# The first FFN part's gate and value products, from SBUF copies to work in their PSUM banks

## The chip, the cores and the metric

The kernel runs on one core of one Trainium2 chip. The time is that of one execution on the device, in microseconds (us). A change below about 0.5% (7.6 us) can hardly be told from none here.

## What is computed

One inference step of a decoder layer on 1032 tokens (a prompt of 1024 and 8 single samples), d_model 1024, everything in fp32. Four recurrent mixers (S5, mLSTM, GLA, RWKV-7) work side by side on 256 channels each, then a gated feed-forward network (FFN) with a causal depthwise convolution of width 3 on the gate. The change touches the FFN alone, whose reference is

```python
h2 = rmsnorm(x, norm_ffn)
up = (h2 @ ffn_w_up).astype(F32)            # 1024 -> 2*2816
ug, uv = jnp.split(up, 2, axis=-1)
padded = jnp.concatenate([ffn_buf.astype(F32), ug], axis=1)
conv = ffn_conv_b.astype(F32)
for j in range(CONV_W):
    conv = conv + ffn_conv_w[j] * padded[:, j:j + T]
ffn = (jax.nn.gelu(conv) * uv) @ ffn_w_down # 2816 -> 1024
x = x + ffn.astype(x.dtype)
```

## The kernel before

**Products.** Activations are kept feature-major: 128 features on the partitions, tokens along the row. An fp32 product is made of three passes in a shorter format (`mm3`, L1123): weights and activations are each split into a high part and a rest, and TensorE adds wh·high (L1129), wh·rest (L1130) and wl·high (L1131) in one PSUM bank. A weight block (128 x 1024) is loaded and split by `load_w`: an SP DMA, a cast on ACT (L1111), four subtractions on POOL (L1112), two buffers of each kind. Activations are split by `split_act`: a cast on ACT (L1120), a subtraction on DVE (L1121).

**Stages.** The tokens go in two segments, 0 to 512 and 512 to 1032. The mixers of the first segment run first, with the input products. Then comes the first FFN part, `ffn(k,0,512,...)`, together with the mixers of the second segment (`SEQ1`); TensorE does FFN work where the mixers leave it free. When the mixers are done (the last mixer matmul is at 981 us) the first FFN part is finished, and the second segment's output product and FFN (`gate_last`) follow, up to the end.

**The first FFN part.** 22 blocks of 128 hidden features, j = 0 to 21. For each, `gate_first` makes a gate product and a value product (`up`, 24 matmuls of 512 columns each) and returns the gated value, which `split_act` splits for the down product; `down(n)` multiplies the blocks by groups of four and adds to the residual `xa` (L1295). `gate_first` before:

- three SBUF tiles from the pool "t" (`tt`, 5 slots): `acc`, `t`, `qr`;
- the gate product in bank `p`; ACT writes the convolution's first tap and the bias to `acc` (L1306), DVE adds the two others from the bank (L1307, twice), ACT keeps the last two columns (L1308);
- the value product in bank `q`; ACT copies it to `qr` (L1310), POOL multiplies it by `acc` (L1311);
- the gelu's gate, `gelu_gate`: Square on ACT (L124), two DVE steps (L125, L126), a sigmoid of three ACT steps (L119 to L121);
- DVE multiplies the two (L1313) into `acc`, which is returned; then L1120 and L1121.

**PSUM.** The FFN and the other big products take banks in turn from a pool of three (`psg`, tag "g"); the other five banks belong to the mixers (`psm`, tags ma, mb, mc).

**Order.** The program is written with priorities (`PRI`: mixers before FFN, and weight loads by a count of their own); a scheduler of the framework puts each engine's instructions into one fixed order at build time, by its own estimate of when they are ready. An instruction waits on its engine, and all behind it on that engine wait too.

Of the kernel before, what the change touches and what calls it, by code (L numbers as in the profile page):

```python
# [8 lines left out]
AF=mybir.ActivationFunctionType; ALU=mybir.AluOpType; PSUM=bass.MemoryType.PSUM; DRAM=bass.MemoryType.DRAM  # L9
# [107 lines left out]
def sigmoid_(k,o,scale=-1.0):  # L117
    A=k.nc.scalar
    A.activation(out=o,in_=o,func=AF.Exp,scale=scale)  # L119
    A.activation(out=o,in_=o,func=AF.Ln,bias=k.eps[0:o.shape[0],2:3])  # L120
    A.activation(out=o,in_=o,func=AF.Exp,scale=-1.0)  # L121
def gelu_gate(k,t,x):

    k.nc.scalar.activation(out=t,in_=x,func=AF.Square,scale=0.044715**.5)  # L124
    k.nc.vector.scalar_tensor_tensor(out=t,in0=t,scalar=1.0,in1=x,op0=ALU.add,op1=ALU.mult)  # L125
    k.nc.vector.tensor_scalar(out=t,in0=t,scalar1=-27.0,scalar2=None,op0=ALU.max)  # L126
    sigmoid_(k,t,-1.5957691216057308)
def v1(k,name,i): 
    c=VC[name]+i
    return k.vec[:,c:c+1]  # L130
# [968 lines left out]
def load_w(k,src,tags=None):  # L1099

    nc=k.nc; k.wn+=1
    if tags: r=k.wp.tile([128,1024],F32,tag="wr",name="wr",bufs=k.wb[0]); h,l=[k.ga.tile([128,1024],F32R,tag=n,name=n) for n in tags]
    elif k.w3 and k.wn%3==0: r,h,l=[k.ga.tile([128,1024],t,tag=n,name=n) for n,t in (('p0',F32),('p1',F32R),('p2',F32R))]
    else: r,h,l=[k.wp.tile([128,1024],t,tag=n,name=n,bufs=b) for n,t,b in zip(('wr','wh','wl'),(F32,F32R,F32R),k.wb)]
    shp=src.shape; n=int(np.prod(shp[1:]))
    def view(t):
        v=t[:,0:n]
        return v if len(shp)==2 else v.rearrange("p (a b)->p a b",a=shp[1]) if len(shp)==3 else v.rearrange("p (c a b)->p c a b",c=shp[1],a=shp[2])
    with k.pr('S'):
        nc.sync.dma_start(out=view(r),in_=src)  # L1110
        nc.scalar.copy(h[:,0:n],r[:,0:n])  # L1111
        for c in range(0,n,256): nc.gpsimd.tensor_tensor(out=l[:,c:c+256],in0=r[:,c:c+256],in1=h[:,c:c+256].bitcast(F32),op=ALU.subtract)  # L1112
    return view(h),view(l)

def tt(k): return k.tp.tile([128,HW],F32,tag="t",name="t",bufs=k.tb)
# [17 lines left out]
def chunks(N):  # L1133
    return [(0,N)] if N<=512 else [(0,N//2),(N//2,N)]
# [44 lines left out]
def split_gain(k,N,i,x,gname):  # L1179
    h=htile(k,i); g=v1(k,gname,i)  # L1180
    k.nc.scalar.activation(out=h[:,0,0:N],in_=x,func=AF.Identity,scale=g)  # L1181
    k.nc.vector.scalar_tensor_tensor(out=h[:,1,0:N],in0=x,scalar=g,in1=h[:,0,0:N].bitcast(F32),op0=ALU.mult,op1=ALU.subtract)  # L1182
    return h

def split_norm(k,N,i,x,r,gname):

    t=tt(k)[:,0:N]; k.nc.gpsimd.tensor_tensor(out=t,in0=x,in1=r[:,0:N],op=ALU.mult)
    return split_gain(k,N,i,t,gname)
# [91 lines left out]
def ffn(k,c0,c1,x2,rs,last=False,then=None):  # L1280
    nc=k.nc; V=nc.vector; A=nc.scalar; GP=nc.gpsimd; N=c1-c0
    NP=N-8
    hs=[split_gain(k,N,i,x2[i][:,0:N],'nffn') if last else split_norm(k,N,i,x2[i][:,0:N],rs.rstd(),'nffn') for i in range(8)]; ms=None if last else Ms(k,N)
    ch=chunks(N); o=2*last
    hid={}
    def down(n):
        ph=[hid.pop(j) for j in range(max(4*n-o,0),min(4*n-o+4,22))]; end=n==5; nm=8//len(ph)
        wd=lambda i,tags=None: load_w(k,(k.wdn,k.wdl)[last][max(4*n-o,0)+i].rearrange("p (m k c)->p m k c",m=nm,c=128),tags)
        if last and end: return ffn_last(k,c0,x2,ch,ph,[wd(0),wd(1),wd(2,("h0","h1")),wd(3,("h2","h3"))])
        for m in range(8):  # L1290
            if m%nm==0: w=wd(m//nm)
            for a,b in ch:
                p=gps(k)
                mm3(k,p[:,0:b-a],(w[0][:,m%nm],w[1][:,m%nm]),ph,a,b)
                V.tensor_tensor(out=x2[m][:,a:b],in0=x2[m][:,a:b],in1=p[:,0:b-a],op=ALU.add)  # L1295
            if end: ms.add(x2[m][:,0:N])
    def up(w):
        ps=[]
        for a,b in ch:
            p=gps(k); ps.append(p)  # L1300
            mm3(k,p[:,0:b-a],w,hs,a,b)
        return ps
    def gate_first(j,wg,wv):

        acc=tt(k); t=tt(k); qr=tt(k); p=up(wg)[0]
        A.activation(out=acc[:,0:N],in_=p[:,0:N],func=AF.Identity,scale=v1(k,'cw2',j),bias=v1(k,'cb',j))  # L1306
        for o,n in ((1,'cw1'),(2,'cw0')): V.scalar_tensor_tensor(out=acc[:,o:N],in0=p[:,0:N-o],scalar=v1(k,n,j),in1=acc[:,o:N],op0=ALU.mult,op1=ALU.add)  # L1307
        A.copy(k.halo[:,j],p[:,N-2:N])  # L1308
        q=up(wv)[0]
        A.copy(qr[:,0:N],q[:,0:N])  # L1310
        GP.tensor_tensor(out=qr[:,0:N],in0=acc[:,0:N],in1=qr[:,0:N],op=ALU.mult)  # L1311
        gelu_gate(k,t[:,0:N],acc[:,0:N])
        V.tensor_tensor(out=acc[:,0:N],in0=qr[:,0:N],in1=t[:,0:N],op=ALU.mult)  # L1313
        return acc
    def gate_last(j,wg,wv):
        g=k.tp.tile([128,HW+2],F32,tag="t",name="t",bufs=k.tb); acc=tt(k)
        pg=up(wg); r=rs.rstd()
        for (a,b),p in zip(ch,pg): V.tensor_tensor(out=g[:,2+a:2+b],in0=p[:,0:b-a],in1=r[:,a:b],op=ALU.mult)  # L1318
        pv=up(wv)
        A.activation(out=acc[:,0:N],in_=g[:,2:2+N],func=AF.Identity,scale=v1(k,'cw2',j),bias=v1(k,'cb',j))  # L1320
        GP.tensor_copy(g[:,0:2],k.halo[:,j])
        V.scalar_tensor_tensor(out=acc[:,0:NP],in0=g[:,1:1+NP],scalar=v1(k,'cw1',j),in1=acc[:,0:NP],op0=ALU.mult,op1=ALU.add)
        V.scalar_tensor_tensor(out=acc[:,0:NP],in0=g[:,0:NP],scalar=v1(k,'cw0',j),in1=acc[:,0:NP],op0=ALU.mult,op1=ALU.add)
        V.tensor_tensor(out=acc[:,NP:N],in0=acc[:,NP:N],in1=k.sdec[:,j],op=ALU.add)
        GP.tensor_copy(k.fcd[:,j],g[:,2+NP:2+N])
        GP.tensor_copy(k.halo[:,j],g[:,NP:NP+2])
        A.activation(out=acc[:,0:N],in_=acc[:,0:N],func=AF.Gelu_apprx_tanh)
        if j==21: k.tc.keep_in_program_order(A.preload_act_table_set("natural_log_exp_and_others"))
        GP.tensor_tensor(out=acc[:,0:N],in0=acc[:,0:N],in1=r[:,0:N],op=ALU.mult)
        for (a,b),q in zip(ch,pv): V.tensor_tensor(out=acc[:,a:b],in0=acc[:,a:b],in1=q[:,0:b-a],op=ALU.mult)  # L1330
        return acc

    for j in range(22):
        wg=load_w(k,k.wup[j,0]); wv=load_w(k,k.wup[j,1])
        acc=(gate_last if last else gate_first)(j,wg,wv)
        u="p%d"%(j-14 if last and j>18 else j%5); h=(k.xb if u>"p4" else k.ga).tile([128,2,HW],F32R,tag=u,name=u)
        split_act(k,h,N,acc[:,0:N]); hid[j]=h
        if j==21 if last and j>=18 else j%4==o and j: down(min((j-1)//4,4))
        if j==1 and then: then()
    if last: return down(5)  # L1340
    def rest():
        now=k.psg,k.tp,k.tb; k.psg,k.tp,k.tb=own[:3]
        down(5); own.append(ms.rstd())
        k.psg,k.tp,k.tb=now
    own=[k.psg,k.tp,k.tb]
    return rest,lambda: ffn_end(k,c0,c1,x2,own[3])

def ffn_last(k,c0,x2,ch,ph,w):

    nc=k.nc; V=nc.vector; A=nc.scalar  # L1350
    def out(a,b,ms):
        n=b-a; r=ms.rstd()
        with k.pr('G'): mul(a,b,n,r)
    def mul(a,b,n,r):
        for m in range(8):
            if m%2==0: t=k.tp.tile([128,2,n],F32,tag="yo",name="yo",bufs=6)
            x=x2[m][:,a:b]; o=t[:,m%2]
            if m in(1,4,6): nc.gpsimd.tensor_tensor(out=o,in0=x,in1=r[:,0:n],op=ALU.mult)
            else: V.scalar_tensor_tensor(out=o,in0=x,scalar=v1(k,'nfin',m),in1=r[:,0:n],op0=ALU.mult,op1=ALU.mult)  # L1359
            if m%2: nc.sync.dma_start(out=k.yT[(m-1)*128:(m+1)*128,c0+a:c0+b].rearrange("(m p) c->p m c",p=128),in_=t)  # L1360
    done=None; ch=((0,LC),(LC,ch[-1][1]))
    for a,b in ch:
        n=b-a; ms=Ms(k,n,2); ms.o=tt(k)
        for m in range(8):
            p=gps(k); x=x2[m][:,a:b]
            mm3(k,p[:,0:n],(w[m//2][0][:,m%2],w[m//2][1][:,m%2]),ph,a,b)
            V.tensor_tensor(out=x,in0=x,in1=p[:,0:n],op=ALU.add)
            ms.add(x)
            if m in(1,4,6): A.activation(out=x,in_=x,func=AF.Identity,scale=v1(k,'nfin',m))
            if done and m==TA: out(*done)  # L1370
        if done: out(a,b,ms)
        done=a,b,ms
# [175 lines left out]
```

## Time and profile before

| | |
|---|---|
| median of 3 runs | 1527.59 us (1526.1 to 1533.52) |
| profiled execution | 1526.3 us, of which the span is 1524.5 us |
| mean granted TensorE clock | 0.967 |
| TensorE busy | 1431.6 us, 94% |
| VectorE (DVE), ScalarE (ACT), GpSimd (POOL) busy | 967.5, 668.9, 918.7 us |
| first FFN part beside the mixers | about 600 to 981 us |
| rest of the first FFN part alone | 981 to 1100 us |

In the rows of the profile, PE is TensorE's matmuls and PEld its weight loads, `g` a tile of the FFN's three banks, `ma` and `mb` tiles of the mixers' banks, `t` one of the SBUF tiles above, `p` a split activation block, `r...`, `b2e` and the like tiles of the mixers. A group's row gives the line, engine, operation, output and inputs, count, then busy time and mean duration, then the engine's idle time just before them with what ended it.

### The profile page before, as it was taken

To read this page: it belongs to the slowest core of one execution; us is meant where nothing else is said; L and a number is where in the kernel's file an instruction comes from. 1 tells how busy PE (TensorE), PEld (TensorE's weight loads), DVE (VectorE), ACT (ScalarE), POOL (GpSimd) and SP (SyncE) were. 2 spreads that over 40 slices of the span, in tenths; PEclk is the share of its full clock that TensorE was granted. 3 is DMA by queue.
4 is the path that set the end of the run, shared out by engine and by line. 5 is a ranking of instruction groups with operands and counts; after the bars stand their busy time and mean duration, and the time that the engine had idled before them with its cause. 6 is when DMAs were issued, how large, how long until landed. Compare 5 with 4: busy or idle time off the path is not lost.

```text
span 1524.5 us, 26739 instructions
## 1 busy us (share of the span) xinstructions
PE 1431.6 (94%) x10113; PEld 1250.3 (82%) x10113; DVE 967.5 (63%) x1987; ACT 668.9 (44%) x1111; POOL 918.7 (60%) x1153
## 2 busy tenths in 40 slices
PE   8688999998999888999899999999999999999997
PEld 6577788887998666767677678788999999999997
DVE  8998847884687947889785774533436434343434
ACT  6135354635373444663644634444542323232333
POOL 8545446545263544664754665866877767576764
PEclk9899999998999999999999999999999999999999
DMA  6455346543354522532224443443334323233232
GB/s 223 161 157 166 110 140 201 175 94 90 103 157 123 158 64 70 162 118 83 77 70 122 120 125 91 136 136 97 113 110 139 92 89 97 87 95 98 86 98 84
DMA packets 110805, 179.80 MB, mean 118 GB/s; under 512 B 33556, under 2 KB 67732, under 8 KB 110676
## 3 DMA queue, kind: packets, MB, share of 16 engines
q1 hardware_dynamic: 110676, 178.08, 38.3%
q8 instruction: 80, 1.31, 0.4%
q14 instruction: 49, 0.40, 0.1%
HBM read 148.10 MB, written 28.41 MB: 116 GB/s over the span
## 4 chain that ended last, share of the span: by engine, by line
PE 45%; DVE 13%; POOL 2%; issue 2%; ACT 2%; DMA 2%; SPq 0%; DVEq 0%; POOLq 0%; ACTq 0%
PE g L1129 14%; PE g L1130 14%; PE g L1131 14%; POOL wl L1112 1%; DVE r L242 1%; DVE r_rs L243 1%; DMA r_rc<-rcD 1%; DVE b4c L515 1%; DVE t L125 1%; DVE h L1182 0%; DVE t L1378 0%; PE mb L395 0%; DVE t L1307 0%; DMA b4b<-MD 0%; DVE yo L1359 0%
## 5 line engine op out<-in xcount | busy, mean ns | idle before, releaser
L1112 POOL TENSOR_TENSOR wl<-wr,wh 128x256 fp32r<-128x256 f32 x708 | 587.1, 861 | 305.9 <-ACT wh L1111 283.5
L1130 PE MATMUL g<-h,wh 128*128 128x260 f32 (+1 forms) x1536 | 493.0, 322 | 5.1 <-DVE h L1182 5.1
L1129 PE MATMUL g<-h,wh 128*128 128x260 f32 (+1 forms) x1536 | 492.9, 322 | 2.0 <-ACT h L1181 1.2
L1131 PE MATMUL g<-h,wl 128*128 128x260 f32 (+1 forms) x1536 | 492.2, 321 | 2.5 <-POOL wl L1112 2.3
L1111 ACT CAST wh<-wr 128x1024 fp32r<-128x1024 f32 x177 | 185.1, 1046 | 299.3 <-PE g L1130 164.2
L1130 PEld LDWEIGHTS g<-h,wh 128*128 128x128 f32 x1536 | 290.7, 189 | 30.5 <-DVE h L1182 8.8
L1131 PEld LDWEIGHTS g<-h,wl 128*128 128x128 f32 x1536 | 291.1, 190 | 27.0 <-POOL wl L1112 5.3
L1129 PEld LDWEIGHTS g<-h,wh 128*128 128x128 f32 x1536 | 290.2, 189 | 26.6 <-issue 2.0
L1129 PE MATMUL g<-p,wh 128*128 128x260 f32 (+1 forms) x496 | 163.0, 329 | 4.6 <-DVE xa L1295 2.5
L1131 PE MATMUL g<-p,wl 128*128 128x260 f32 (+1 forms) x496 | 161.6, 327 | 2.2 <-POOL wl L1112 2.2
L1130 PE MATMUL g<-p,wh 128*128 128x260 f32 (+1 forms) x496 | 162.9, 329 | 0.0
L1129 PEld LDWEIGHTS g<-p,wh 128*128 128x128 f32 x496 | 94.7, 191 | 14.6 <-DVE xa L1295 2.9
L1131 PEld LDWEIGHTS g<-p,wl 128*128 128x128 f32 x496 | 94.4, 191 | 10.7 <-POOL wl L1112 2.7
L1130 PEld LDWEIGHTS g<-p,wh 128*128 128x128 f32 x496 | 94.5, 190 | 8.0 <-issue 0.6
L1112 POOL TENSOR_TENSOR p<-p,p 128x256 fp32r<-128x256 f32 x76 | 61.7, 841 | 51.3 <-ACT p L1111 48.8
L1295 DVE TENSOR_TENSOR xb<-xb,g 128x260 f32<-128x260 f32 x80 | 33.6, 424 | 59.2 <-PE g L1131 59.2
L1295 DVE TENSOR_TENSOR xa<-xa,g 128x512 f32<-128x512 f32 x48 | 32.8, 683 | 34.6 <-PE g L1131 34.5
L1318 DVE TENSOR_TENSOR t<-g,r 128x260 f32<-128x260 f32 x44 | 18.6, 424 | 56.2 <-PE g L1131 51.3
L1307 DVE SCALAR_TENSOR_TENSOR t<-g,vec,t 128x511 f32<-128x511 f32 (+1 forms) x44 | 32.7, 743 | 27.3 <-ACT t L1306 27.1
L1129 PE MATMUL g<-h,p 128*128 128x260 f32 (+1 forms) x144 | 49.6, 344 | 0.0
L1130 PE MATMUL g<-h,p 128*128 128x260 f32 (+1 forms) x144 | 49.3, 342 | 0.0
L1131 PE MATMUL g<-h,p 128*128 128x260 f32 (+1 forms) x144 | 49.3, 342 | 0.0
(718 smaller groups left out, 2741.7 us busy)
## 6 DMA issues: line engine op xcount, KB each, us to landing
wr<-in_wup_dram SPq DMA_DIRECT2D x88, 512.0 KB
wr<-in_wfm_dram SPq DMA_DIRECT2D x27, 512.0 KB
wr<-in_wdn_dram SPq DMA_DIRECT2D x22, 512.0 KB
wr<-in_wdl_dram SPq DMA_DIRECT2D x22, 512.0 KB
wr<-in_wout_dram SPq DMA_DIRECT2D x13, 512.0 KB
p<-in_wfm_dram SPq DMA_DIRECT2D x11, 512.0 KB
t<-in_xT_dram SPq DMA_DIRECT2D x16, 260.0 KB
b4c<-B8Td SPq DMA_DIRECT2D x6, 512.0 KB
```

Of the source, the lines that this page charges most:

```text
L125: k.nc.vector.scalar_tensor_tensor(out=t,in0=t,scalar=1.0,in1=x,op0=ALU.add,op1=ALU.mult)
L242: V.tensor_tensor(out=tv,in0=bc(Ls[:,jj+1:32,jj:jj+1],[128,n,m]),in1=bc(X[:,jj:jj+1,0:m],[128,n,m]),op=ALU.mult)
L243: V.tensor_tensor(out=X[:,jj+1:32,0:m],in0=X[:,jj+1:32,0:m],in1=tv,op=ALU.subtract)
L515: V.scalar_tensor_tensor(out=W[:,hp,cc,j],in0=Mb[:,h,cc],scalar=k.tok[:,qi+cc,0,h:h+1],in1=k.mbig,op0=ALU.subtract,op1=ALU.max)
L1111: nc.scalar.copy(h[:,0:n],r[:,0:n])
L1112: for c in range(0,n,256): nc.gpsimd.tensor_tensor(out=l[:,c:c+256],in0=r[:,c:c+256],in1=h[:,c:c+256].bitcast(F32),op=ALU.subtract)
L1129: T.matmul(out,wh[:,i],a,start=i==0,stop=False)
L1130: T.matmul(out,wh[:,i],b,start=False,stop=False)
L1131: T.matmul(out,wl[:,i],a,start=False,stop=i==n-1)
L1295: V.tensor_tensor(out=x2[m][:,a:b],in0=x2[m][:,a:b],in1=p[:,0:b-a],op=ALU.add)
L1307: for o,n in ((1,'cw1'),(2,'cw0')): V.scalar_tensor_tensor(out=acc[:,o:N],in0=p[:,0:N-o],scalar=v1(k,n,j),in1=acc[:,o:N],op0=ALU.mult,op1= ...
L1318: for (a,b),p in zip(ch,pg): V.tensor_tensor(out=g[:,2+a:2+b],in0=p[:,0:b-a],in1=r[:,a:b],op=ALU.mult)
```

## The change

The Square's result goes to the gate's bank `p` instead of to the SBUF tile, and the product behind it reads it there. The copy of the value product and its tile are gone: POOL multiplies `acc` by the finished sigmoid, and DVE multiplies that by the value product in its bank `q`, in place. `gate_first` returns the bank, so that the split's cast and subtraction read PSUM. Arithmetic changes only in the order of two multiplications. The second FFN part (`gate_last`) is not changed.

```diff
-def gelu_gate(k,t,x):
+def gelu_gate(k,t,x,s=None):
+    s=t if s is None else s
-    k.nc.scalar.activation(out=t,in_=x,func=AF.Square,scale=0.044715**.5)
-    k.nc.vector.scalar_tensor_tensor(out=t,in0=t,scalar=1.0,in1=x,op0=ALU.add,op1=ALU.mult)
+    k.nc.scalar.activation(out=s,in_=x,func=AF.Square,scale=0.044715**.5)
+    k.nc.vector.scalar_tensor_tensor(out=t,in0=s,scalar=1.0,in1=x,op0=ALU.add,op1=ALU.mult)
     k.nc.vector.tensor_scalar(out=t,in0=t,scalar1=-27.0,scalar2=None,op0=ALU.max)
     sigmoid_(k,t,-1.5957691216057308)
...
     def gate_first(j,wg,wv):
-        acc=tt(k); t=tt(k); qr=tt(k); p=up(wg)[0]
+        acc=tt(k); t=tt(k); p=up(wg)[0]
...
         q=up(wv)[0]
-        A.copy(qr[:,0:N],q[:,0:N])
-        GP.tensor_tensor(out=qr[:,0:N],in0=acc[:,0:N],in1=qr[:,0:N],op=ALU.mult)
-        gelu_gate(k,t[:,0:N],acc[:,0:N])
-        V.tensor_tensor(out=acc[:,0:N],in0=qr[:,0:N],in1=t[:,0:N],op=ALU.mult)
-        return acc
+        gelu_gate(k,t[:,0:N],acc[:,0:N],p[:,0:N])
+        GP.tensor_tensor(out=t[:,0:N],in0=acc[:,0:N],in1=t[:,0:N],op=ALU.mult)
+        V.tensor_tensor(out=q[:,0:N],in0=t[:,0:N],in1=q[:,0:N],op=ALU.mult)
+        return q
```

Lines 123 to 1303 of before are one higher after the change. The scheduler makes a new order of it. It differs from before's between the first FFN product and the end of the first FFN part; behind that the two programs run alike. Three places:

On ACT, one block near the end of the first FFN part. Before (L1306 first tap, L1308 last columns, L1111 a weight cast, L1310 the copy, L124 the Square, L119 to L121 the sigmoid):

```order
L1306 ACTIVATE t<-g,vec 128x512
L1308 COPY halo<-g 128x2
L1111 CAST wh<-wr 128x1024
L1310 COPY t<-g 128x512
L124 ACTIVATE t<-t 128x512
L119 ACTIVATE t<-t 128x512
L120 ACTIVATE t<-t,eps 128x512
L121 ACTIVATE t<-t 128x512
```

After (L1121 is the split's cast of the block before):

```order
L1307 ACTIVATE t<-g,vec 128x512
L1121 CAST p_7585<-g 128x512
L1309 COPY halo<-g 128x2
L125 ACTIVATE g<-t 128x512
L1112 CAST wh<-wr 128x1024
L119 ACTIVATE t<-t 128x512
L120 ACTIVATE t<-t,eps 128x512
L121 ACTIVATE t<-t 128x512
```

The copy is gone, the Square writes a bank `g`, and it stands ahead of the weight cast instead of behind it.

On PE, beside the mixers, the end of a product of the fourth block and the start of the next product. Before (g_6153 takes the next bank in turn):

```order
L1129 MATMUL g_6095<-h7_5780,wh_6055 128x512
L1130 MATMUL g_6095<-h7_5780,wh_6055 128x512
L1131 MATMUL g_6095<-h7_5780,wl_6056 128x512
L1129 MATMUL g_6153<-h0_5745,wh_6133 128x512
L1130 MATMUL g_6153<-h0_5745,wh_6133 128x512
```

After, in two pieces (g_6144 is the same product, and takes over the bank of g_6003, the third block's value product; L822 and L821 are the S5 mixer's products):

```order
L1130 MATMUL g_6088<-h7_5780,wh_6049 128x512
L1131 MATMUL g_6088<-h7_5780,wh_6049 128x512
L1132 MATMUL g_6088<-h7_5780,wl_6050 128x512
L822 MATMUL mb_9271<-b4e_9206,b2e_9254 64x128
L822 MATMUL mb_9272<-b4e_9206,b2e_9254 64x128
```

```order
L822 MATMUL mb_9271<-b4e_9206,b2e_9254 64x128
L822 MATMUL mb_9272<-b4e_9206,b2e_9254 64x128
L1130 MATMUL g_6144<-h0_5745,wh_6125 128x512
L1131 MATMUL g_6144<-h0_5745,wh_6125 128x512
L1132 MATMUL g_6144<-h0_5745,wl_6126 128x512
```

The next product started directly behind the one before it, and the mixer's products stood inside it; now they stand ahead of it.

On DVE, the release of that bank (the third place). Before (L1307 a tap of the fourth block, L1121 the third block's split):

```order
L96 TENSOR_TENSOR r_5_9565<-ma_9561,r_6_9564 128x512
L1307 SCALAR_TENSOR_TENSOR t_6063<-g_6066,vec_95,t_6063 128x510
L812 COPY s_X_9242<-b2e_9298 128x2x4
L1121 TENSOR_TENSOR p2_6042<-t_5976,p2_6042 128x512
L201 TENSOR_TENSOR r_KR_9582<-r_xa_9496,r_34_9536 128x4x64 x2
```

After:

```order
L175 COPY r_f_9508<-r_f_9508 128x2
L1308 SCALAR_TENSOR_TENSOR t_6057<-g_6059,vec_95,t_6057 128x510
L813 COPY s_X_9198<-b2e_9254 128x2x4
L1122 TENSOR_TENSOR p2_6036<-g_6003,p2_6036 128x512
L96 TENSOR_TENSOR r_5_9521<-ma_9517,r_6_9520 128x512
```

The split's subtraction reads the bank g_6003 instead of an SBUF tile, and stands ahead of the mixer's L96, which was three rows ahead of it before.

## The prediction

> **What bounds the kernel now.** I read the page's engine sums and slices first, then the busy time by stretch, then the chain of waits and the waits of the two stretches in which TensorE has gaps, and last the groups of instructions there.
>
> ```profile
> PE 1431.6 (94%) x10113; PEld 1250.3 (82%) x10113; DVE 967.5 (63%) x1987; ACT 668.9 (44%) x1111; POOL 918.7 (60%) x1153
> ...
> PE   8688999998999888999899999999999999999997
> ...
> DVE  8998847884687947889785774533436434343434
> ```
>
> TensorE (PE) is busy for 94% of the 1524.5 us span. A change on ACT, DVE and POOL can gain only where PE has gaps, or lose by making new ones. A slice is 38 us; the changed function works in the slices 17 to 29 (600 to 1085 us), where DVE's row stands at 7 to 9 up to 800 us and at 3 to 5 from 915 us. The busy time by stretch (columns: window, its length, busy time of PE, weight load, DVE, ACT and POOL with instructions, granted clock, DMA share, GB/s) says where the gaps are:
>
> ```profile
> 620.00:765.00 145.00, 132.61 (x765) 99.84 (x765) 123.52 (x218) 83.18 (x138) 88.83 (x102) 0.94 0.33 102
> 765.00:975.00 210.00, 200.61 (x1183) 157.88 (x1181) 142.00 (x262) 100.68 (x192) 130.68 (x138) 0.97 0.36 107
> 975.00:1085.00 110.00, 110.00 (x543) 92.07 (x542) 45.53 (x68) 48.08 (x73) 74.19 (x86) 1.00 0.39 124
> ```
>
> From 620 to 765 us PE lacks 12.4 us and DVE is busy for 123.5 of 145. From 765 to 975 PE lacks 9.4 us, with DVE at 142 of 210. From 975 on PE lacks nothing. So 12.4 + 9.4 = 21.8 us is all that the change can win, and the last third of the function's products can win nothing. The chain of waits in the two stretches:
>
> ```profile
> by line: issue 9.2%; DVE r L242 6.7%; DMA r_rc<-rcD 6.3%; DVE r_rs L243 5.6%; DVE t L125 4.5%; DVE xa L1295 2.9%; DVE t L1307 2.7%; DVE t L1313 2.7%; DVE r_xa L149 2.5%; PE g L1129 2.4%; PE g L1130 2.2%; DVE b2c L804 2.0%; PE g L1131 1.9%;
> by line: PE g L1131 15.1%; PE g L1130 14.9%; PE g L1129 14.3%; POOL wl L1112 8.2%; issue 5.3%; DVE d_xm L988 2.0%; DVE b4c L515 1.9%; PE mb L395 1.9%; DMA d_xm<-in_sh_dram 1.7%; ACT wh L1111 1.5%; DMA DV<-r_KB 1.2%; POOL t L1311 1.2%; POOL
> ```
>
> In the first row the chain is DVE's queue, the mixers' operations (L242, L243) with the FFN's (L125, L1313) between them; PE's filler products are under 7%. In the second row PE's own products lead, and of the FFN's DVE steps none is among the lines printed. What PE waits for from 620 to 765 (us, times, longest):
>
> ```profile
> PE ma L289 <- DVE r_KB L286: 3.3, 1, 3.3
> PE mb L335 <- DVE b4d L115: 2.4, 1, 2.4
> PE ma L210 <- DVE r_KB L199: 1.5, 1, 1.5
> PE mb L821 <- DVE b2e L810: 1.3, 1, 1.3
> ```
>
> These are mixer results that come late from DVE. A cheaper FFN step on DVE brings them forward only as far as it stands ahead of them in DVE's queue.
>
> **The change part by part.** Line numbers are those of before. *DVE operands.* L125's product, L1313 and the split's subtraction L1121 have one operand in SBUF and one in PSUM, where they had two in SBUF. Their groups from 620 to 765 (count | busy us, mean ns | idle before):
>
> ```profile
> L125 DVE SCALAR_TENSOR_TENSOR t<-t 128x512 f32<-128x512 f32 x6 | 9.5, 1590 | 3.1 <-ACT t L124 3.1
> L1313 DVE TENSOR_TENSOR t<-t 128x512 f32<-128x512 f32 x6 | 6.5, 1080 | 3.6 <-ACT t L121 3.3 <-POOL b4d L838 0.3
> L1295 DVE TENSOR_TENSOR xa<-xa,g 128x512 f32<-128x512 f32 x8 | 5.4, 676 | 0.0
> L1121 DVE TENSOR_TENSOR p<-t,p 128x512 fp32r<-128x512 f32 x5 | 5.0, 998 | 0.0
> L1307 DVE SCALAR_TENSOR_TENSOR t<-g,vec,t 128x511 f32<-128x511 f32 x6 | 4.5, 747 | 3.7 <-ACT t L1306 3.7
> L1310 ACT COPY t<-g 128x512 f32<-128x512 f32 x6 | 3.5, 577 | 0.0
> L1311 POOL TENSOR_TENSOR t<-t 128x512 f32<-128x512 f32 x6 | 8.5, 1410 | 0.8 <-DVE s_X L812 0.8
> L1112 POOL TENSOR_TENSOR wl<-wr,wh 128x256 fp32r<-128x256 f32 x64 | 56.4, 913 | 32.6 <-ACT wh L1111 23.4 <-issue 8.3 <-DVE b2d L800 0.7
> ```
>
> L1307 has the form that L125 gets (one operand from a bank) and takes 747 ns; L1295 is the same for the two TENSOR_TENSOR and takes 676. So an L125 should save 1590 - 747 = 843 ns, an L1313 404 ns, an L1121 322 ns. The spread of the two forms over the whole program (min/median/max) says why the means differ:
>
> ```profile
> L125 DVE SCALAR_TENSOR_TENSOR t<-t x22: 674/1018/4656, 609.1 to 1071.7; 128x512 f32<-128x512 f32 x22
> L1307 DVE SCALAR_TENSOR_TENSOR t<-g,vec,t x44: 727/748/751, 602.8 to 1066.3; 128x511 f32<-128x511 f32 x22, 128x510 f32<-128x510 f32 x22
> ```
>
> The form with a bank is steady. The one with two SBUF operands can be quicker (674) or as slow as 4656. [...]
>
> On the path: L125 is 4.5% of 145 us = 6.5 us of the chain, and loses 843/1590 of it: **-3.5**. L1313 is 2.7% = 3.9 us, and loses 404/1080: **-1.5**. L1121 is below the last entry printed, so under 1.9% = 2.8 us, and a third of that is 0.9 at most: **-0.5**. From 765 to 975 the same steps are nearer to their floor:
>
> ```profile
> L125 DVE SCALAR_TENSOR_TENSOR t<-t 128x512 f32<-128x512 f32 x10 | 10.2, 1024 | 10.6 <-ACT t L124 10.6
> ...
> L1121 DVE TENSOR_TENSOR p<-t,p 128x512 fp32r<-128x512 f32 x10 | 8.0, 800 | 1.6 <-ACT p L1120 1.6
> L1313 DVE TENSOR_TENSOR t<-t 128x512 f32<-128x512 f32 x10 | 7.8, 779 | 4.6 <-ACT t L121 4.6
> ...
> L1310 ACT COPY t<-g 128x512 f32<-128x512 f32 x10 | 5.8, 575 | 0.0
> ```
>
> They are idle before they start, and none is on the chain with 1.2% or more: **-0.5**, at most the 2.8 + 1.2 + 1.0 = 5.0 us that the three groups would shed down to 747 and 676 ns.
>
> *The ACT copy.* 577 ns less per product on ACT, which is busy for 83 of 145 us and is not on the printed chain. PE's waits from 600 to 975 have it once, with 0.3 us:
>
> ```profile
> PE g L1131 <- POOL wl L1112: 4.0, 3, 2.2
> ...
> PE g L1129 <- ACT t L1310: 0.3, 1, 0.3
> ```
>
> By itself I cost it at nothing. It lets the Square, which stood behind it, start earlier: L125 is idle for 3.1 us before six starts, waiting for the Square, and of these I take **-1.0** (bounds: nothing, and 3.1).
>
> *POOL's product* moves from beside the sigmoid to behind it. It is then a link of its own, 1410 ns. A product's path from its value matmul to the split becomes 1.41 - 0.84 - 0.40 - 0.32 - 0.58 = 0.7 us shorter when nothing else stands in POOL's queue. What does stand there is weight splitting: the row of L1112 has 56.4 us of 145, in runs of four of 0.91 us.
>
> *The banks.* The FFN has three. The value bank q was free after the copy and is now held to the split's subtraction; the gate bank p was free after the halo copy and is now held to the product behind the Square. Counted on the two orders between the first FFN product and the last mixer, 18 products now start in a bank that a DVE step of this chain has to release, and whose start no earlier instruction of PE had already made to wait for it; before, 10 starts hung so on the copy or the convolution, which were long done. Behind a PE product that waits stand the mixers' matmuls in PE's queue, and DVE waits for those. Does the release come in time? One place of the loaded stretch, the third product (j=2): its value product ends, the split's subtraction runs, and PE reaches the matmul that stands, in the new order, where the bank is needed again.
>
> ```profile
> 636.36 0.39 PE L1131 MATMUL g<-h,wl 128*128 128x512 f32 x1
> ...
> 660.05 0.68 DVE L1121 TENSOR_TENSOR p<-t,p 128x512 fp32r<-128x512 f32 x1
> ...
> 661.61 0.74 PE L100 MATMUL ma<-r,cfr 128*128 128x512 f32 x2
> ```
>
> Released at 660.73 and needed at 661.61: by the clock of before it fits by 0.9 us. A place behind the mixers, where PE has no gaps:
>
> ```profile
> 1012.82 0.39 PE L1131 MATMUL g<-h,wl 128*128 128x512 f32 x1
> ...
> 1021.46 0.69 DVE L1121 TENSOR_TENSOR p<-t,p 128x512 fp32r<-128x512 f32 x1
> ...
> 1024.15 0.40 PE L1129 MATMUL g<-h,wh 128*128 128x512 f32 x1
> ```
>
> The last value matmul ends at 1013.2, the subtraction at 1022.15, the third bank's turn is at 1024.15: it fits by 2.0 us. So I take the ties as met at most of the 18 places and missed at one in five, by the 0.9 us of the nearer row: 4 x 0.9 = **+3.6**. The ends are nothing and, at each place, a whole run of four weight splittings plus POOL's product less that slack, 3.65 + 1.41 - 0.9 = 4.2 us.
>
> The **sum**, against the profiled execution's 1526.3 us (span 1524.5 and 1.8 around it; it lies 1.3 under the median of the three runs): -3.5 - 1.5 - 0.5 - 0.5 - 1.0 + 3.6 = -3.4, so **1523**.
>
> **The rivals.** *The ties win (slower).* POOL's product as last link stands behind weight splitting. With that at 56.4/145 = 39% of POOL's time and half a run of four (1.8 us) left on average, it starts 0.7 us late, and with the 1.41 us of its own less the slack of 0.9 each of the 18 starts is late by 1.2 us: 21.7 us of PE, less the relief of 7.0 above, gives 1526.3 + 14.7 = **1541**. It decides from (7.6 + 7.0)/18 = 0.8 us per place. For it: three banks only, a release that took 24 us at the quoted place, and 0.9 us of slack there. Against it: the path gets shorter by 0.7 us, and at 1013 to 1024 it fits with PE at full speed. [...]
>
> *All of DVE's relief counts (faster).* Where DVE's queue leads, each nanosecond off it brings a mixer forward. The three groups shed 6 x 0.843 + 6 x 0.404 + 5 x 0.322 = 9.1 us in the first stretch and 5.0 in the second, 14.1 in all, with ties that are met: **1512**. With four of the 9.3 us of ACT's copies besides it is 1508. For it: DVE at 85% from 620 to 765, and the four waits above, all for DVE. Against it: the chain has only 10.4 us of L125 and L1313 in it, and issue, DMA and the mixers' recurrence hold the rest.
>
> *The bank operand isn't cheaper.* If the three steps keep their means, only the copy is gone and the ties of +3.6 stay: **1530**. The steady 747 ns of L1307 speak against it. It could be that DVE then merely waits elsewhere, as POOL's and ACT's queues do.
>
> **How the numbers follow.** Forecast (1515 to 1531) 0.42, all relief 0.30, ties win 0.20, not cheaper 0.08. A difference under 0.5%, 7.6 us, is about what a measurement of this kernel can't tell from no change, so "faster" is below 1518.7 and "slower" above 1533.9. Faster is the 0.30 and 0.05 of the forecast's lower end; slower the 0.20; the rest, 0.45, lies between. The range reaches from the second rival's low end, 1508, to the first rival's price, 1541.
>
> **What would show it.** Right: L125, L1313 and L1121 near 750 and 680 ns with no long ones; PE's lack from 600 to 975 a few us below 21.8; new waits of PE's products on DVE's subtraction or on the product behind the Square, a handful of 1 us each. Wrong to the slow side: those waits on most of the 18 places, and POOL's product idle behind weights ahead of them. Wrong to the fast side: the four mixer waits gone. The forecast fails altogether if the time moves behind 975 us, where PE has no gap, or if the other order of the mixers, which I cost at nothing because nearly as many FFN matmuls (2712 after, 2719 before) are issued by the last mixer matmul, opens gaps of its own.

## The result, and the profile after

The changed kernel takes 1516.09 us (median of 11 runs, 1508.87 to 1524.14) against 1526.76 for before (11 runs): a ratio of 0.9932, 95% interval 0.9909 to 0.9955, some 10.4 us less. The forecast was 1523, that is 3.4 us less than the profiled run of before. The measured time lies inside the forecast's range (1515 to 1531) by 1.1 us only. The profiled execution of after has a span of 1517.6 us, 6.9 less than before's.

The busy time by stretch, of after (columns as in the prediction):

```profile
620.00:765.00 145.00, 133.21 (x789) 100.06 (x789) 119.73 (x235) 83.97 (x141) 87.57 (x104) 0.96 0.35 109
765.00:975.00 210.00, 204.14 (x1214) 161.76 (x1209) 132.35 (x260) 98.00 (x183) 127.12 (x146) 1.00 0.36 111
975.00:1085.00 110.00, 110.00 (x546) 92.49 (x545) 39.70 (x63) 48.04 (x70) 66.95 (x86) 1.00 0.40 128
```

In equal windows TensorE (PE) gets 24 and 31 matmuls more done than before. Its busy time rises by 4.1 us in all, and the granted clock rises from 0.94 to 0.96 and from 0.97 to 1.00. To compare like with like, the two kernels are cut at the same places of the program: at the first matmul of the first FFN part and at the last mixer matmul. First before's three stretches, then after's:

```profile
0.00:596.40 596.40, 538.31 (x3998) 459.34 (x3998) 454.10 (x1085) 279.11 (x498) 312.57 (x414) 0.95 0.46 139
596.40:981.30 384.90, 363.12 (x2118) 282.10 (x2118) 286.54 (x521) 196.15 (x352) 236.88 (x260) 0.96 0.35 104
981.30:1524.50 543.20, 530.12 (x3999) 508.82 (x3999) 226.90 (x382) 193.69 (x261) 369.30 (x480) 1.00 0.34 104
```

```profile
0.00:600.00 600.00, 541.10 (x3998) 460.65 (x3999) 457.64 (x1085) 278.87 (x498) 314.24 (x414) 0.94 0.46 138
600.00:971.20 371.20, 353.55 (x2111) 275.26 (x2110) 262.10 (x521) 188.79 (x335) 219.83 (x258) 0.99 0.36 108
971.20:1517.60 546.40, 533.46 (x4006) 511.47 (x4006) 224.61 (x383) 191.99 (x257) 363.64 (x481) 0.99 0.33 104
```

The first stretch is the same work in both kernels and took 3.6 us longer after. The changed stage is 13.7 us shorter. The last one is 3.2 us longer: it has the 7 matmuls left over and a little less clock. In the changed stage PE lacks 17.7 us instead of 21.8, which is 4.1 us of the 13.7; the other 9.6 us are PE's own busy time, for 7 matmuls fewer (1.6 us) at a clock of 0.99 instead of 0.96. So in this profile most of the gain of the stage lies in the clock. A second profile of the change (`a2_change_again`, below) lacks 17.8 us in its stage (373.3 us, PE busy for 355.51).

The chain of waits from 620 to 765 us, after (lines are one higher than before):

```profile
by line: issue 7.9%; DVE r L243 7.0%; DMA r_rc<-rcD 6.6%; DVE r_rs L244 6.3%; PE g L1130 4.1%; PE g L1131 3.5%; DVE t L1308 3.4%; DMA r_KB<-r_KB 3.3%; PE g L1132 3.3%; DVE b2c L805 2.5%; DVE xa L1296 2.1%; POOL wl L1113 2.0%; ACT wh L1112 2
```

L126 (L125 before) and L1313, 4.5% and 2.7% of it before, are no longer among the entries; PE's products, under 7% before, are 10.9%. The groups from 600 to 975 us, first before's and then after's:

```profile
L125 DVE SCALAR_TENSOR_TENSOR t<-t 128x512 f32<-128x512 f32 x17 | 20.8, 1226 | 17.5 <-ACT t L124 17.4
L1313 DVE TENSOR_TENSOR t<-t 128x512 f32<-128x512 f32 x16 | 14.3, 892 | 8.2 <-ACT t L121 7.9 <-POOL b4d L838 0.3
L1121 DVE TENSOR_TENSOR p<-t,p 128x512 fp32r<-128x512 f32 x16 | 13.7, 855 | 1.6 <-ACT p L1120 1.6
```

```profile
L1313 DVE TENSOR_TENSOR g<-t,g 128x512 f32<-128x512 f32 x17 | 11.8, 693 | 8.5 <-POOL t L1312 8.5
L126 DVE SCALAR_TENSOR_TENSOR t<-g,t 128x512 f32<-128x512 f32 x17 | 11.6, 684 | 2.9 <-ACT g L125 2.9
L1122 DVE TENSOR_TENSOR p<-g,p 128x512 fp32r<-128x512 f32 x17 | 11.6, 683 | 0.7 <-ACT p L1121 0.5
```

The three DVE steps take 35.0 us instead of 48.8, and the product behind the Square waits 2.9 us for it instead of 17.5. Ahead of the last product stand 8.5 us of waiting for POOL's. Among PE's waits from 600 to 975 the new ones are

```profile
PE g L1130 <- DVE t L126: 3.0, 2, 1.7
...
PE g L1130 <- DVE p L1122: 1.9, 2, 1.2
...
PE g L1132 <- POOL wl L1113: 0.5, 2, 0.3
```

that is four missed bank ties, 4.9 us, while the waits for POOL's weights fall from 4.0 to 0.5 us.

The means hide one instruction. Before, a single L125 took 4.66 us, beside products of POOL that followed each other without a pause, and the mixer's L286 stood behind it in DVE's queue. PE's longest gap of the stage followed (rows of DVE, then of POOL, then of PE):

```profile
755.71 4.66 DVE L125 SCALAR_TENSOR_TENSOR t<-t 128x512 f32<-128x512 f32 x1
...
762.73 0.43 DVE L286 TENSOR_SCALAR r_KB<-ma 64x256 f32<-64x256 f32 x1
...
756.05 1.27 POOL L1311 TENSOR_TENSOR t<-t 128x512 f32<-128x512 f32 x1
757.29 1.27 POOL L350 TENSOR_TENSOR b2e<-b2e,b4a 128x512 f32<-128x512 f32 x1
758.53 1.28 POOL L353 TENSOR_TENSOR b2f<-b2f,b4a 128x512 f32<-128x512 f32 x1
...
763.21 1.22 PE L289 MATMUL ma<-r_KB,r 128*128 128x128 f32 x4 [3.28 <-DVE r_KB L286]
```

The trace's clock record has half speed from 762.0 for 6.83 us, of which PE worked 5.6, so the gap and the slow clock behind it cost 3.3 + 2.8 = 6.1 us at this one place. In both profiles of the change no DVE step between 735 and 770 us takes more than 1.6 us, and PE doesn't wait for this mixer step.

### The profile page after: what moved, and what is told of

Its sections match the earlier page's. It is cut to its first block, busy times and chain, and to the rows that moved or that the text cites. A ratio compares the mean times of both kernels' runs of the same rounds, so it can differ in the third digit from the quotient of the medians.

```text
span 1517.6 us, 26716 instructions
## 1 busy us (share of the span) xinstructions
PE 1428.1 (94%) x10113; PEld 1247.4 (82%) x10113; DVE 944.3 (62%) x1987; ACT 659.7 (43%) x1089; POOL 897.7 (59%) x1153
## 4 chain that ended last, share of the span: by engine, by line
PE 46%; DVE 12%; POOL 2%; DMA 2%; ACT 2%; issue 2%; SPq 0%; DVEq 0%; POOLq 0%; ACTq 0%
PE g L1130 14%; PE g L1131 14%; PE g L1132 14%; POOL wl L1113 1%; DVE r L243 1%; DVE r_rs L244 1%; DMA r_rc<-rcD 1%; DVE t L1308 1%; DVE h L1183 0%; DVE t L1378 0%; DVE b4c L516 0%; DMA b4b<-MD 0%; DVE yo L1359 0%; ACT wh L1112 0%; DMA r_KB<-r_KB 0%
## 5 line engine op out<-in xcount | busy, mean ns | idle before, releaser
L1113 POOL TENSOR_TENSOR wl<-wr,wh 128x256 fp32r<-128x256 f32 x708 | 566.2, 830 | 306.5 <-ACT wh L1112 277.7
L1132 PE MATMUL g<-h,p 128*128 128x260 f32 (+1 forms) x144 | 48.8, 339 | 0.0
L1131 PE MATMUL g<-h,p 128*128 128x260 f32 (+1 forms) x144 | 48.8, 339 | 0.0
L1308 DVE SCALAR_TENSOR_TENSOR t<-g,vec,t 128x511 f32<-128x511 f32 (+1 forms) x44 | 32.7, 742 | 23.9 <-ACT t L1307 23.7
```

Of the source, the lines that this page charges most:

```text
L1131: T.matmul(out,wh[:,i],b,start=False,stop=False)
L1132: T.matmul(out,wl[:,i],a,start=False,stop=i==n-1)
```

## The experiments

Theories: **A**, cheaper DVE steps of the FFN shorten PE's gaps and with them the spells at half clock. **B**, the copy and the tile that are gone let the scheduler find a better order. **C**, banks held longer and POOL's late product cost time that the rest hides. **D**, on record ahead of the last four runs only: what matters is POOL's early product, which runs freely beside DVE. Each ratio is to before on the same chip; the 95% intervals reach 0.13 to 0.22% to either side, so differences under the 0.5% named at the start can be told apart here. Line numbers in the texts on record and below are each kernel's own.

**The halves of the change.** `e1_square_bank` keeps before's copy, early product and last product, and writes only the Square to the bank:

```diff
-        gelu_gate(k,t[:,0:N],acc[:,0:N])
+        gelu_gate(k,t[:,0:N],acc[:,0:N],p[:,0:N])
```

> Only the Square goes to the gate's bank; the value product is copied and multiplied as before the change. Theory A (cheaper DVE steps shorten TensorE's gaps, and with them the spells at half clock): the product behind the Square at about 0.69 us in place of 1.23, 8 of the 14 us that the three DVE steps gave up, so about half of the change's gain: ratio to before about 0.996 (0.994 to 0.999), 4 to 5 half-clock spells between the first FFN product and the last mixer matmul where before has 6 and the change 3. Theory B (the copy and the tile that are gone let the scheduler find a better order): no gain, 0.999 to 1.002, 6 spells.

1525.61 us, ratio 1.0029 (1.0013 to 1.0045): slower. Both theories failed. From 600 to 975 us:

```profile
L1314 DVE TENSOR_TENSOR t<-t 128x512 f32<-128x512 f32 x17 | 22.7, 1335 | 8.4 <-ACT t L121 5.4 <-POOL t L1312 3.0
...
L1122 DVE TENSOR_TENSOR p<-t,p 128x512 fp32r<-128x512 f32 x16 | 14.1, 880 | 0.8 <-ACT p L1121 0.7
L126 DVE SCALAR_TENSOR_TENSOR t<-g,t 128x512 f32<-128x512 f32 x17 | 11.6, 683 | 2.4 <-ACT g L125 2.4
```

The product behind the Square became as short as forecast, and the last product grew from 892 to 1335 ns: the three steps together take 48.4 us, about as before (48.8). What one step gave, the next that reads two SBUF tiles took. Some 3.7 of the last product's 8.4 us more are again one instruction, near the same place, and the same product of PE waits behind it:

```profile
753.86 4.64 DVE L1314 TENSOR_TENSOR t<-t 128x512 f32<-128x512 f32 x1 [1.52 <-ACT t L121]
...
760.22 1.22 PE L290 MATMUL ma<-r_KB,r 128*128 128x128 f32 x4 [3.95 <-DVE r_KB L287]
```

`e2_value_bank` is the other half: the change with the Square left in SBUF.

```diff
-        gelu_gate(k,t[:,0:N],acc[:,0:N],p[:,0:N])
+        gelu_gate(k,t[:,0:N],acc[:,0:N])
```

> Only the value side: no copy, POOL's product behind the sigmoid, DVE's product and the split in the value's bank; the Square stays in SBUF. Theory A: the product behind the Square keeps about 1.2 us, the other two fall to 0.69; 6 of the 14 us of DVE, ratio 0.996 to 0.999. Theory B: nearly all of the gain, 0.992 to 0.995, since copy and tile are gone. Theory C (POOL's product as last link and the value bank held longer cost time, hidden in the change by the Square's gain): 1.000 to 1.004.

1517.15 us, 0.9962 (0.9948 to 0.9975). About half of the gain, at the value that A gave; the value bank missed three ties for 7.9 us, one of them for 6.2.

`e3_sbuf_result` is the change with the last product in SBUF, so that the bank is free earlier:

```diff
-        V.tensor_tensor(out=q[:,0:N],in0=t[:,0:N],in1=q[:,0:N],op=ALU.mult)
-        return q
+        V.tensor_tensor(out=acc[:,0:N],in0=t[:,0:N],in1=q[:,0:N],op=ALU.mult)
+        return acc
```

> As the change, but DVE's last product goes to the SBUF tile acc, so that the value bank is free one cast and one subtraction (1.3 us) earlier and the split reads SBUF again. Theory A: the split's subtraction goes back to about 0.85 us, 3 of the 14 us of DVE are lost: ratio to before 0.993 to 0.996, a little slower than the change. Theory C (the banks' ties cost): the 1.9 us that TensorE waits for the split in the change are gone, 0.990 to 0.993.

1514.04 us, 0.9946 (0.9929 to 0.9963). PE's waits for the split's subtraction fall from 1.9 to 0.2 us, the split goes back to 885 ns, and the ratio is where A had it: the early release shows no gain over the change. It is no clean test of the ties, though: in this order one mixer step of DVE stood for 6.97 us beside POOL, and PE waited 4.2 us behind it, which the change doesn't have (a row of DVE's, and one of PE's waits):

```profile
744.30 6.97 DVE L382 TENSOR_TENSOR b4e<-b4e,b4d 128x512 f32<-128x512 f32 x1 [0.58 <-POOL b4d L358]
...
PE ma L290 <- DVE r_KB L287: 4.2, 1, 4.2
```

`e4_pool_last` is before with POOL's product behind the sigmoid, all operands in SBUF and the copy kept:

```diff
-        GP.tensor_tensor(out=qr[:,0:N],in0=acc[:,0:N],in1=qr[:,0:N],op=ALU.mult)
         gelu_gate(k,t[:,0:N],acc[:,0:N])
+        GP.tensor_tensor(out=t[:,0:N],in0=acc[:,0:N],in1=t[:,0:N],op=ALU.mult)
```

> The kernel before with one edit: POOL multiplies acc by the finished sigmoid, so that its product is the last link before DVE's; copy, tile and all SBUF operands stay. Theory A: no DVE relief; the link makes the block's path 1.4 us longer, but no bank hangs on it, so it shows only where a down product waits for the split: ratio 0.999 to 1.003. Theory B: the order changes a little, 0.998 to 1.002. Theory C: 1.003 or more.

1517.87 us, 0.9972 (0.9959 to 0.9985): faster by 4.3 us, which no theory had as its own value (B's range just reaches it). The FFN's three DVE steps take 18.2 + 16.4 + 16.2 = 50.8 us for 51 instructions, 1.00 us each as before (48.8 for 49). So a part of the gain comes without any bank operand.

**Order and slots.** `a2_change_again` is the changed kernel unaltered.

> The changed kernel again, unaltered, beside before on the same chip, for a second profile of the same program. If the half-clock spells of one profile belong to the program, the stage from the first FFN product to the last mixer matmul has 2 to 4 of them again (the first profile had 3, before 6). If they are an accident of the execution, their number is anywhere from 2 to 6, and the mean clock of the runs lies near before's 0.970. Ratio 0.991 to 0.996 by both.

1514.38 us, 0.9930 (0.9911 to 0.9949). The stage has 4 half-clock spells in the trace's clock record (3 in the first profile of the change, 6 before), 17.1 us long where the two had 10.2 and 30.7. The mean clock of its runs is 0.973; that of the 11 first runs of the change is 0.9715; that of before 0.970 (25 runs), 0.970 (23) and 0.970 (11). The spells of a profile are partly its own accident. The mean of 0.973 against 0.970 on the same chip is clear of the scatter of its runs (0.972 to 0.974) and so the program's; the 0.9715, from runs of 0.967 to 0.977, isn't by itself.

`f1_third_tile` gives the changed kernel back its third tile, and `e7_six_slots` gives before a sixth slot:

```diff
-        acc=tt(k); t=tt(k); p=up(wg)[0]
+        acc=tt(k); t=tt(k); qr=tt(k); p=up(wg)[0]
...
-        GP.tensor_tensor(out=t[:,0:N],in0=acc[:,0:N],in1=t[:,0:N],op=ALU.mult)
-        V.tensor_tensor(out=q[:,0:N],in0=t[:,0:N],in1=q[:,0:N],op=ALU.mult)
+        GP.tensor_tensor(out=qr[:,0:N],in0=acc[:,0:N],in1=t[:,0:N],op=ALU.mult)
+        V.tensor_tensor(out=q[:,0:N],in0=qr[:,0:N],in1=q[:,0:N],op=ALU.mult)
```

> The change with one edit: POOL's product goes to a third tile of the pool t, so that a block takes 3 of the 5 slots as before; every operation has the operand kinds of the change. Theory A (cheaper DVE steps): as the change, 0.991 to 0.996. Theory B (the free slots give a better order): back to 0.998 to 1.002.

```diff
-TB=5
+TB=6
```

> Before with 6 slots in the pool t in place of 5: two whole blocks fit. The same instructions and operands. Theory A: no DVE relief, 0.998 to 1.002. Theory B with the slots as the cause: 0.992 to 0.996, most of the gain of the change.

1511.33 us, 0.9913 (0.9892 to 0.9935), and 1525.61 us, 1.0009 (0.9994 to 1.0024). The slots are not the cause, from either side.

`f2_gelu_first` is before with the gelu's gate written ahead of the copy and POOL's product, the same instructions in another order:

```diff
+        gelu_gate(k,t[:,0:N],acc[:,0:N])
         A.copy(qr[:,0:N],q[:,0:N])
         GP.tensor_tensor(out=qr[:,0:N],in0=acc[:,0:N],in1=qr[:,0:N],op=ALU.mult)
-        gelu_gate(k,t[:,0:N],acc[:,0:N])
```

> Before with the code of the gelu's gate ahead of the copy and POOL's product: the same instructions on the same operands, in another order (Square ahead of the copy). Theory A: no DVE relief, so the order alone moves it by noise: 0.998 to 1.002. Theory B (any other order of the stage is worth some tenths of a per cent): anything from 0.995 to 1.005, and the DVE groups keep their means near 1.2, 0.9 and 0.86 us.

1529.27 us, 1.0030 (1.0016 to 1.0044), above A's range. An earlier Square alone wins nothing. And order alone moves this kernel by 0.3%, as much as single edits above do: an edit's difference of that size isn't yet its own mechanism.

**Without POOL's product.** `f3_no_pool_product` is before with copy and product replaced by one DVE product from the bank:

```diff
-        A.copy(qr[:,0:N],q[:,0:N])
-        GP.tensor_tensor(out=qr[:,0:N],in0=acc[:,0:N],in1=qr[:,0:N],op=ALU.mult)
+        V.tensor_tensor(out=qr[:,0:N],in0=acc[:,0:N],in1=q[:,0:N],op=ALU.mult)
```

> Before with the copy and POOL's product replaced by one DVE product that reads the value bank (acc times value, to the tile qr); the Square, the product behind it, the last product and the split stay in SBUF. DVE gets one instruction of about 0.69 us more per block, 12 us in the stage. Theory A (what counts is the FFN's DVE time): slower than before, 1.002 to 1.008. Theory D (POOL's early product, running freely beside DVE, blocks DVE's two-operand steps, the mixers' too): the mixers' DVE instructions of the stage fall from 200 to about 193 us as in e4_pool_last, and the ratio is 0.993 to 0.999.

1517.29 us, 0.9959 (0.9943 to 0.9975). From 600 to 975 us:

```profile
L1312 DVE TENSOR_TENSOR t<-t 128x512 f32<-128x512 f32 x17 | 18.2, 1068 | 8.0 <-ACT t L121 7.8
L1121 DVE TENSOR_TENSOR p<-t,p 128x512 fp32r<-128x512 f32 x17 | 15.2, 897 | 2.3 <-ACT p L1120 2.2
L125 DVE SCALAR_TENSOR_TENSOR t<-t 128x512 f32<-128x512 f32 x17 | 15.0, 883 | 4.9 <-ACT t L124 4.8
...
L1310 DVE TENSOR_TENSOR t<-t,g 128x512 f32<-128x512 f32 x17 | 11.6, 682 | 9.6 <-PE g L1131 9.6
```

The FFN's steps on DVE take 60.0 us instead of 48.8, and the kernel is faster. Theory A, as the sum of the FFN's DVE time, falls here; D had the ratio and the mixers' time (192.9 us) right.

`e5_dve_product` is the change with POOL's late product on DVE, `e6_early_bank_product` the change with an early DVE product in the value bank in place of POOL's late one, and `g1_third_tile_sbuf_result` is `f1_third_tile` with the last product in `acc`, as in `e3_sbuf_result`:

```diff
-        GP.tensor_tensor(out=t[:,0:N],in0=acc[:,0:N],in1=t[:,0:N],op=ALU.mult)
+        V.tensor_tensor(out=t[:,0:N],in0=acc[:,0:N],in1=t[:,0:N],op=ALU.mult)
```

> The change with POOL's product (acc times the sigmoid) done by DVE, both operands in SBUF: POOL does only weights and mixers, and the chain of a block has no POOL link (1.3 us). Theory A: DVE has 17 products of 0.7 to 1.2 us more in the stage, 12 to 20 us, the relief of the bank operands is spent: 0.997 to 1.001. Theory C (the link through POOL holds the value bank): 0.988 to 0.992. Theory D: in between, 0.992 to 0.996, as the mixers' DVE time stays near 193 us.

```diff
+        V.tensor_tensor(out=q[:,0:N],in0=acc[:,0:N],in1=q[:,0:N],op=ALU.mult)
         gelu_gate(k,t[:,0:N],acc[:,0:N],p[:,0:N])
-        GP.tensor_tensor(out=t[:,0:N],in0=acc[:,0:N],in1=t[:,0:N],op=ALU.mult)
```

> The change with POOL's product replaced by an early DVE product in the value bank (value times acc, then times the sigmoid at the end): three bank steps and no POOL link behind the sigmoid. DVE has 17 x 0.69 = 12 us more than the change. Theory A: 0.996 to 1.000. Theory C: 0.989 to 0.993. Theory D: 0.992 to 0.996.

```diff
-        V.tensor_tensor(out=q[:,0:N],in0=qr[:,0:N],in1=q[:,0:N],op=ALU.mult)
-        return q
+        V.tensor_tensor(out=acc[:,0:N],in0=qr[:,0:N],in1=q[:,0:N],op=ALU.mult)
+        return acc
```

> f1_third_tile with the last product written to the SBUF tile acc in place of the value bank: the bank is free 1.3 us earlier, the split reads SBUF. Theory A: 0.992 to 0.995 (3 us of DVE lost against f1_third_tile's 0.9913). Theory C: 0.988 to 0.991, the best of all. No theory puts it above 0.997.

1514.06 us, 0.9931 (0.9911 to 0.9952); 1509.00 us, 0.9903 (0.9888 to 0.9918); and 1518.01 us, 0.9955 (0.9940 to 0.9970). The first came at D's value. The second is the fastest kernel measured, at the value of C and below D's; its interval just overlaps the change's. The third went against C: releasing the bank earlier again won nothing, and against the kernel it was made from it lost 0.4%. It has the mixer step of 6.96 us and PE's wait of 4.2 us that `e3_sbuf_result` has.

All in one table. "POOL early" says whether POOL multiplies ahead of the sigmoid. "FFN steps" is the sum of the FFN's elementwise DVE products and the split beside the mixers, of groups like those quoted, from 600 to 975 us (16 or 17 blocks); "mixers" is the sum of the durations of 381 mixer instructions of DVE (all but the six of the mixers' own gelu) between the first FFN product and the last mixer matmul, worked out from the trace's records (380 in `e7_six_slots`).

| kernel | POOL early | FFN steps us | mixers us | ratio |
|---|---|---|---|---|
| before | yes | 48.8 | 200.3 | 1 |
| f2_gelu_first | yes | 45.1 | 203.6 | 1.0030 |
| e1_square_bank | yes | 48.4 | 201.0 | 1.0029 |
| e7_six_slots | yes | 48.1 | 200.6 | 1.0009 |
| e4_pool_last | no | 50.8 | 193.5 | 0.9972 |
| e2_value_bank | no | 43.4 | 192.4 | 0.9962 |
| f3_no_pool_product | no product | 60.0 | 192.9 | 0.9959 |
| g1_third_tile_sbuf_result | no | 35.5 | 200.7 | 0.9955 |
| e3_sbuf_result | no | 38.1 | 196.5 | 0.9946 |
| e5_dve_product | no product | 49.7 | 193.6 | 0.9931 |
| the change (again) | no | 35.0 | 193.7 (191.8) | 0.9932 (0.9930) |
| f1_third_tile | no | 34.9 | 198.4 | 0.9913 |
| e6_early_bank_product | no product | 46.6 | 189.0 | 0.9903 |

The four kernels in which POOL multiplies early lie at 1.000 to 1.003, the nine without at 0.990 to 0.997. No other column separates them so. Single long waits do it only in part. A DVE step of 4.6 to 8.7 us between 735 and 770 us stands in the profiles of all four of the first, but also in those of `f1_third_tile`, `f3_no_pool_product`, `e3_sbuf_result` and `g1_third_tile_sbuf_result` (4.9 to 7.0); in the other five kernels the longest there is 2.2 us.

## Why the prediction was right in its direction and short in its size

The sum gave 3.4 us and the measurement 10.4. That the time still lies in the range is partly luck: it is 1.1 us from the edge, and below the 1518.7 under which the prediction speaks of "faster", an outcome it gave 0.35.

**DVE operands: right.** The three steps were put at 747, 676 and 676 ns; they take 684, 693 and 683. Their spread over the program, of after:

```profile
L126 DVE SCALAR_TENSOR_TENSOR t<-g,t x22: 671/684/693, 609.3 to 1062.0; 128x512 f32<-128x512 f32 x22
L1313 DVE TENSOR_TENSOR g<-t,g x22: 674/695/785, 616.3 to 1068.8; 128x512 f32<-128x512 f32 x22
```

The longest L126 is 0.69 us where L125 had one of 4.66. Why the form with a bank has no long ones, no run shows by itself. What the prediction didn't see is that relief at one step can return at the next: `e1_square_bank` shortened L126 from 1226 to 683 ns, and the last product took up nearly all of it (from 892 to 1335 ns). And it spread over a mean what was mostly one instruction: of the 6.5 us that it gave L125 on the chain, 4.7 are the L125 at 755.71.

**What PE lacks: right in sum, less so by its terms.** Forecast -7.0 of relief and +3.6 of ties, so -3.4; the stage lacks 4.1 us less (4.0 in the second profile). The ties missed at four places, as forecast, for 4.9 us. Of the relief behind it, some 9 us, 3.5 are waits for POOL's weights, which the sum left out; without them it is 5.5. Those 3.5 may belong to before's order: the other three kernels with POOL's early product wait 1.4 (`f2_gelu_first`), 0.8 (`e1_square_bank`) and 0.4 us (`e7_six_slots`) for them. Of the four mixer waits that the prediction lists, 8.5 us, the same products still wait 4.0. Whether the ties are a toll on top is open: where they were loosened (`e3_sbuf_result`, `g1_third_tile_sbuf_result`) the kernel got no faster, but both have the new mixer wait of 4.2 us.

**The ACT copy and the early Square: not shown as a gain.** The wait for the Square fell from 17.5 to 2.9 us, yet `f2_gelu_first`, which also brings the Square forward, is slower.

**POOL's move: the step that was mis-sized.** The prediction has it as a link of 1.41 us in the path, a cost in the sum of the path and the core of the slower rival. On its own (`e4_pool_last`) it makes the kernel 4.3 us faster, the interval 2.3 to 6.2 (0.9959 to 0.9985 of 1522.92). That is no more than order alone moved (0.3%); what speaks for it is that all nine kernels without the early product lie below all four with it, and that D had two of its three ratios right ahead of the runs. The remaining 6 us or so came with the copy's end and the bank operands, which no run separates from the new order; the Square's bank operand with POOL's early product is 0.29% slower. Why the early product costs is not settled. In the one profile of `e4_pool_last` PE lacks no less over the whole span (94.5 us against 92.9), and by the mean clock of the runs 1.7 of its 4.3 us are clock. The mixers' DVE time speaks for theory D in most rows. A single step proves little: L515, from 600 to 975 us, of before and of `e4_pool_last`:

```profile
L515 DVE SCALAR_TENSOR_TENSOR b4c<-b4b,m_tok,cf 128x128 f32<-128x128 f32 x8 | 4.2, 587 | 0.0
```

```profile
L515 DVE SCALAR_TENSOR_TENSOR b4c<-b4b,m_tok,cf 128x128 f32<-128x128 f32 x8 | 2.2, 337 | 0.0
```

But `e1_square_bank` and `f2_gelu_first`, with the early product, have 405 and 340 ns for the same step and are slow; `e2_value_bank` and `f3_no_pool_product`, without it, have 714 and 681 and are fast. And `f1_third_tile` is fast with 198.4 us of mixers, `g1_third_tile_sbuf_result` with 200.7. With order alone worth 0.3%, that the new orders happen to suit the mixers remains possible.

**The clock: left out.** The sum had no term for it. It held PE's gaps, 21.8 us, to be all that the change can win, and the slow clock behind a gap, as at 762.0 (2.8 us there), is won or lost besides. By the mean clock of the runs, (1 - clock) x span is 45 to 46 us for before and 43.1 (11 runs) or 40.8 us (6 runs) for the change: 2 to 5 of its 10 us. The 9.6 us of the one profile overstate it. With 3 us of clock added the sum would have been 1520.

**The rivals.** That the ties win: no, four misses and not eighteen. That the operand isn't cheaper: no. That all relief counts (1512): nearest to the time, though not by its mechanism, since the FFN's DVE time doesn't order the kernels.

## What to carry to other kernels

Take an engine's relief as real only when the next step doesn't take it back (here the last product went from 892 to 1335 ns): make half of the change and look at that step's mean, and at its longest instance, which can carry most of the difference (here 4.7 of the 6.5 us of L125 on the chain). When an operation runs on a second engine, beside a loaded one, may matter more than how long it makes a block's path (here 4.3 us, the reason open). And where the order is a scheduler's, measure one or two neutral reorderings (here 0.3%) before crediting an edit with less.

## What the runs showed of the hardware

Before, TensorE's clock was at half speed behind a gap of 1.49 us that ends at 675.94, so that the price came behind the gap (five-us windows, the column behind POOL is the clock; the trace's clock record has 0.5 from 676.6 for 6.83 us):

```profile
670.00:675.00 5.00, 4.45 (x25) 3.35 (x23) 4.87 (x6) 1.80 (x4) 4.04 (x5) 1.00 0.15 54
675.00:680.00 5.00, 4.06 (x18) 3.70 (x19) 4.68 (x8) 4.52 (x7) 2.51 (x3) 0.66 0.42 156
680.00:685.00 5.00, 5.00 (x44) 3.75 (x43) 3.80 (x7) 3.29 (x6) 3.92 (x4) 0.66 0.34 105
685.00:690.00 5.00, 5.00 (x30) 3.96 (x30) 5.00 (x13) 2.40 (x4) 2.98 (x4) 1.00 0.02 5
```

Ten microseconds at 0.66 are 3.4 us lost, over twice the gap itself. The spells in the clock records of before and after last 3.4, 6.8, 10.2 or 13.7 us, but for the one that the end cuts off. Not every gap has such a spell behind it: of after, PE lacks 2.65 us here and keeps its clock:

```profile
725.00:730.00 5.00, 2.35 (x12) 1.64 (x11) 4.62 (x16) 1.10 (x2) 1.13 (x2) 1.00 0.34 105
730.00:735.00 5.00, 4.71 (x21) 3.53 (x20) 4.65 (x12) 4.27 (x8) 3.63 (x5) 1.00 0.00 0
```

Three long DVE steps with two operands in SBUF ended 0.3 to 0.56 us behind a row of POOL's instructions without a pause, not behind a single one. The L125 of 4.66 us, in before, ends at 760.37, 0.56 us behind the last of POOL's products in a row (759.81). The step of 6.97 us in `e3_sbuf_result` ends at 751.27, 0.56 us behind a row of seven of POOL's that ends at 750.71, and one of 8.65 us in `f2_gelu_first` at 764.13, 0.3 us behind a row of ten. With one operand in a bank the same step never took more than 0.69 us in the change. That POOL's instructions are what held them is argued from these times; no run takes the row away alone.

In all 14 profiles the span, less what PE lacks and less half of the spells in the clock record, is 1380.6 to 1386.7 us. For before that is 1524.5 - 92.9 - 50.2, for the change 1517.6 - 89.5 - 43.5. The spans differ by up to 22.7 us, this rest by 6.1, so lack and clock together make most of the differences between these kernels; between these two they leave 3.2 us out.
